# Two of the seven half-width products of a block, each pass of the large weight parts joined into one 512-column matmul

## The chip, the cores and the metric

The kernel runs on one core of a Trainium2 chip. The metric is the device time of one launch in microseconds (us). Three launches of the kernel before took 1768.8 to 1769.22 us, median 1769.01 us.

The engines are PE (matrix products, into PSUM), DVE (vector), ACT (scalar functions, also plain copies), POOL (GpSimd) and SP, which issues most transfers; POOL issues those transfers that add to what is already there.

## The reference

A decoder trunk of two layers on a 512 x 1024 activation in float32. Each layer is a gated feed-forward block (ffn), a token mixer and a second ffn, so there are four ffns in all, and they hold most of the time:

```python
def swiglu(h, w_gate, w_up, w_down):
    return (jax.nn.silu(h @ w_gate) * (h @ w_up)) @ w_down

for l in range(L):
    x = x + 0.5 * swiglu(rms_norm(x, ffn1_norm[l]), ffn1_w_gate[l], ffn1_w_up[l], ffn1_w_down[l])
    ...   # convolution and differential attention, joined by one output projection
    x = x + 0.5 * swiglu(rms_norm(x, ffn2_norm[l]), ffn2_w_gate[l], ffn2_w_up[l], ffn2_w_down[l])
```

The inner width of an ffn is 2816, that is 22 chunks of 128.

## The kernel before

**Split operands.** Each float32 operand is split in two parts that the PE takes: a high part `hi` (ACT copies it, L101 for weights) and a low part `lo` (DVE subtracts, L102; POOL in a few places of the mixer). A product of a weight chunk and an activation is three matmuls: high by high, high weight by low activation, low weight by high activation. L200, L203 and L204 are these three at 512 columns.

**Seven products.** Where the plain scheme would do eight half-width products, the kernel does seven, on weight combinations and activation combinations. This is done for the up and gate projections (`seven`, 16 of them in an ffn) and for the down projection (`Pair`, 8 in an ffn). The 22 chunks of an ffn are taken in three parts (`PARTS`): six chunks in the plain way at 512 columns, then a part of 8 sevens and 4 pairs, then another of 8 sevens and 4 pairs. So there are 64 sevens and 32 pairs in a launch. At the end of an ffn the first products of what follows begin two activation tiles in, before the last pair is finished (`first_products` with a `tail`), and take the eight tiles of `x` in the order 0, 4, 1, 5, 2, 6, 3, 7.

**One seven.** It has two PSUM banks of 512 columns, each used as two halves of 256: `a`, `d` in `banks[0]` and `b`, `c` in `banks[1]`. A product is four chunks of three matmuls of 256 columns (L434), 12 in all, accumulated in one of the halves; `go` names the half, the weight combination and the activation combination. In program order they are c, d, then `before()`, which is the last product of the seven before it (`rest`, weight `g1u1`), then a, b, c and a (weight `g1u2u1`). Between them ACT copies halves of the banks to the tile `keep` (four slots of 256 columns; L439, L443, L448), so that differences of accumulated states can be taken later, and DVE adds them back in (L451, L456, L457), ACT takes SiLU (L452), and DVE forms the gated product (L460). `Hidden.add` then splits that (L483 on ACT, L484 on DVE) and makes its combinations (L489 to L494).

**One pair** follows the same pattern for the down projection (matmuls at L523): `head`, `body` and `finish`. `finish` does the last product and adds to the running `x` (L572, L573, L574); the body adds its own half at L565 and L566. `finish_halves` serves the very last pair of the launch. After each finished `x` tile, `Prep.tile` splits it for the next products (L308 on ACT, L309 on DVE, L321 for the sum of squares).

**Order.** A scheduler turns the program into one instruction stream per engine; each stream runs in order, with semaphores between engines. Weights pass through rings of SBUF buffers (5 raw, 4 sums, 9 high, 9 low). A group of seven weight combinations is made ahead of its seven: four loads, two sums by a load on SP and a load on POOL's queue that adds to it (L160), two sums on DVE (L175, L176), seven splits (L101 on ACT and L102 on DVE).

Of the kernel before, what the change touches and what calls it, by code (L numbers as in the profile page):

```python
# [11 lines left out]
F32 = mybir.dt.float32  # L12
F32R = mybir.dt.float32r
I32 = mybir.dt.int32
AF = mybir.ActivationFunctionType
# [55 lines left out]
def trunk(ctx: ExitStack, tc: tile.TileContext, xt, par, lamv, relb, onehot,  # L71
# [12 lines left out]
    def f32(ap):  # L84
        return ap.bitcast(F32)
# [120 lines left out]

    x = act.tile([P, KT, SEQ], F32, tag="x", name="x")

    acth = act.tile([P, KT, SEQ], F32R, tag="acth", name="acth")
    actl = act.tile([P, KT, SEQ], F32R, tag="actl", name="actl")  # L210
# [11 lines left out]
    S.activation(small.tile([P, 1], F32, tag="first", name="first", bufs=1), f32(ones_r[:, P : P + 1]), AF.Copy)  # L222
# [152 lines left out]
    class Halves:  # L375
# [4 lines left out]
        def __init__(self, fp, pr, r):  # L380
            self.th = fp.tile([P, 3, KT // 2, HS], F32R, tag="th", name="th")
            self.tl = fp.tile([P, 3, KT // 2, HS], F32R, tag="tl", name="tl")

            self.whole = []
            four = [fp.tile([P, 4, SEQ], F32, tag=tag, name="hn") for tag in ("yh", "yl")]
            free = [t[:, n] for t in four for n in range(4)]
            a, b = slice(0, HS), slice(HS, SEQ)
            for j in range(KT // 2):
                for k in (j, j + KT // 2):
                    h = free.pop()  # L390
                    V.scalar_tensor_tensor(h, x[:, k, :], col(pr.l, pr.gain, k), r, op0=ALU.mult, op1=ALU.mult)
                    self.whole.append((k, h))
                (_, ha), (_, hb) = self.whole[-2:]
                t = fp.tile([P, 3, HS], F32, tag="ht", name="ht", bufs=1)
                V.tensor_tensor(t[:, 1], hb[:, b], ha[:, b], op=ALU.subtract)
                V.tensor_tensor(ha[:, b], ha[:, a], ha[:, b], op=ALU.subtract)
                V.scalar_tensor_tensor(t[:, 0], ha[:, b], -1.0, hb[:, b], op0=ALU.mult, op1=ALU.subtract)
                V.scalar_tensor_tensor(t[:, 2], t[:, 0], -1.0, hb[:, a], op0=ALU.mult, op1=ALU.subtract)
                S.activation(self.th[:, :, j, :], t, AF.Copy)
                V.tensor_tensor(self.tl[:, :, j, :], t, f32(self.th[:, :, j, :]), op=ALU.subtract)  # L400
# [16 lines left out]
    def seven(halves, w, banks, fp, before, last):  # L417
# [7 lines left out]
        g = keep[:, 0::2]  # L425
# [11 lines left out]

        go(c, "u2u1", "t1", first=True)
# [4 lines left out]
        S.activation(keep[:, :2], banks[0].rearrange("p (n c) -> p n c", n=2), AF.Copy)  # L443
        go(b, "g2", "b21")
        if not last:
            go(c, "all", "b22")
        go(a, "g1u2u1", "t2")
        saves.append(S.activation(keep[:, 2], a, AF.Copy))  # L448
        if last:
            go(c, "all", "b22")  # L450
# [14 lines left out]
    class Hidden:  # L465

        def __init__(self, fp, n):
            self.fp, self.n, self.parts = fp, n, [None] * (2 * n)
            self.th = fp.tile([P, 3, n, HS], F32R, tag="yh", name="yh")
            self.tl = fp.tile([P, 3, n, HS], F32R, tag="yl", name="yl")  # L470
# [33 lines left out]
    class Pair:  # L504

        def __init__(self, hid, fp, m, m2):
            self.hid, self.m, self.m2 = hid, m, m2
            self.kc, self.kd = (1, 3) if m == 0 else (3, 1)
            self.banks = pair_banks()
            self.a, self.d = self.banks[0][:, :HS], self.banks[0][:, HS:]  # L510
            self.b, self.c = self.banks[1][:, :HS], self.banks[1][:, HS:]
            self.keep = fp.tile([P, 4, HS], F32, tag="gn", name="keep", bufs=2)
            self.begun = set()
# [19 lines left out]
        def body(self, w, before, more=None, last=False):  # L533
            a, b, c, d, go = self.a, self.b, self.c, self.d, self.go
            both = self.banks[0].rearrange("p (n c) -> p n c", n=2)
            if self.m == 0:
# [13 lines left out]
                saves.append(S.activation(self.keep[:, 2:], both, AF.Copy))  # L550
            else:
# [4 lines left out]
                self.early = S.activation(self.keep[:, :2], both, AF.Copy)  # L556
                go(b, w["g2"], "b21")
                if not last:
                    go(c, w["all"], "b22")
                go(a, w["g1u2u1"], "t2")  # L560
                saves.append(S.activation(self.keep[:, 2], a, AF.Copy))
# [3 lines left out]
            V.tensor_tensor(two, two, self.keep[:, 0::2], op=ALU.add)  # L565
            V.scalar_tensor_tensor(xm, self.banks[1], 0.5, xm, op0=ALU.mult, op1=ALU.add)  # L566
            return nxt

        def finish(self, weight):
            a, d, xn = self.a, self.d, x[:, self.m2, :]  # L570
            self.go(a, weight, "t3")
            V.tensor_tensor(d, a, self.keep[:, self.kc], op=ALU.add)  # L572
            V.tensor_tensor(a, a, self.keep[:, self.kd], op=ALU.add)  # L573
            V.scalar_tensor_tensor(xn, self.banks[0], -0.5, xn, op0=ALU.mult, op1=ALU.add)  # L574

        def finish_halves(self, weight, store):
            a, xs = self.a, x[:, self.m2, :].rearrange("p (n c) -> p n c", n=2)
            V.scalar_tensor_tensor(xs, self.keep[:, 1::2], -0.5, xs, op0=ALU.mult, op1=ALU.add)
# [173 lines left out]
    def make_scalars():  # L752
        for l in range(DEPTH):
# [5 lines left out]
            d = small.tile([P, 2], F32, tag="lamd", name="lamd", bufs=1)  # L759
            V.tensor_reduce(d, pr, axis=AX.X, op=ALU.add)  # L760
            e = small.tile([P, 2], F32, tag="lame", name="lame", bufs=1)
# [428 lines left out]
```

## Time and profile before

| | before |
|---|---|
| median of 3 launches | 1769.01 us |
| profiled launch, its own time | 1769.0 us |
| span of that launch | 1767.2 us |
| PE busy | 1758.8 us, 11852 matmuls |
| DVE busy | 1472.1 us (83% of the span) |
| ACT busy | 1037.1 us (59%) |
| POOL busy | 515.7 us (29%) |

The profiled launch has 1.8 us outside its span and agrees with the median. Instructions on one engine are pipelined, so the durations of rows next to each other overlap a little, and those of matmuls much: a matmul's interval is the distance between starts and not its duration.

### The profile page before, as it was taken

How to read it: one execution, taken by the hardware profiler on the slowest of the kernel's cores; microseconds unless marked ns; L12 is line 12 of the kernel's file. 1: busy time of each engine (PE TensorE's matmuls, PEld its weight loads, DVE VectorE, ACT ScalarE, POOL GpSimd, SP SyncE). 2: the span in 40 equal slices, each digit the busy share in tenths (PEclk: the TensorE clock that was granted, in tenths of full speed). 3: DMA queues.
4: the chain of work that ended last, by engine and by line, in shares of the span. 5: the costliest groups of instructions: out<-in, count | busy, mean ns of one | idle time of the engine just before them, and what ended most of it. 6: DMA issues, size and time to landing. Idle time of an engine off the chain costs nothing.

```text
span 1767.2 us, 32964 instructions
## 1 busy us (share of the span) xinstructions
PE 1758.8 (100%) x11852; PEld 1621.2 (92%) x11852; DVE 1472.1 (83%) x2646; ACT 1037.1 (59%) x1955; POOL 515.7 (29%) x497
## 2 busy tenths in 40 slices
PE   9999999999999999999999999999999999999998
PEld 7799999988788899999988999999887888999998
DVE  7969888969877969989987798999698678698887
ACT  6546566755865436566644565666559554465664
POOL 1011112169970011212200121121798600112122
PEclk9999999999999999999999999999999999999999
DMA  7457777533223457677544576776231234576774
GB/s 229 129 138 185 172 188 190 138 120 100 68 78 114 126 129 178 171 198 179 141 143 111 147 177 172 198 166 166 91 114 49 96 102 139 134 183 163 201 183 127
DMA packets 166613, 257.78 MB, mean 146 GB/s; under 512 B 19271, under 2 KB 63318, under 8 KB 166448
## 3 DMA queue, kind: packets, MB, share of 16 engines
q1 hardware_dynamic: 129600, 201.25, 35.5%
q0 software_dynamic: 36416, 54.12, 18.7%
q8 instruction: 93, 1.52, 0.4%
q14 instruction: 72, 0.59, 0.1%
q10 hardware_dynamic: 432, 0.29, 0.1%
HBM read 253.48 MB, written 3.42 MB: 145 GB/s over the span
## 4 chain that ended last, share of the span: by engine, by line
PE 97%; DVE 1%; POOL 1%; ACT 1%; issue 0%; DVEq 0%; POOLq 0%
PE ps_pair L434 37%; PE ps_pair L523 18%; PE ps_pair L200 9%; PE ps_pair L203 9%; PE ps_pair L204 9%; PE ps_out L200 2%; PE ps_out L203 2%; PE ps_out L204 2%; PE ps_pair L842 2%; PE ps_pair L843 2%; PE ps_pair L841 2%; PE ps_sc L958 1%; PE ps_v L872 1%; PE ps_v L873 1%; PE ps_v L871 1%; POOL wlo L102 0%
## 5 line engine op out<-in xcount | busy, mean ns | idle before, releaser
L101 ACT ACTIVATE whi<-wraw 128x512 fp32r<-128x512 f32 x744 | 452.9, 627 | 397.4 <-PE ps_pair L203 166.3
L102 DVE TENSOR_TENSOR wlo<-wraw,whi 128x512 fp32r<-128x512 f32 x640 | 426.2, 685 | 111.5 <-ACT whi L101 104.2
L160 POOL DMA_DIRECT2D wsum<-in_gu x128 | 112.0, 904 | 700.4 <-DMA wsum<-in_gu 270.7
L434 PE MATMUL ps_pair<-acth,wlo 128*128 128x256 f32 x1024 | 289.8, 283 | 0.0
L434 PE MATMUL ps_pair<-actl,whi 128*128 128x256 f32 x1024 | 289.8, 283 | 0.0
L434 PE MATMUL ps_pair<-acth,whi 128*128 128x256 f32 x1024 | 289.8, 283 | 0.0
L434 PE MATMUL ps_pair<-th,whi 128*128 128x256 f32 x768 | 217.3, 283 | 0.0
L434 PE MATMUL ps_pair<-tl,whi 128*128 128x256 f32 x768 | 217.3, 283 | 0.0
L434 PE MATMUL ps_pair<-th,wlo 128*128 128x256 f32 x768 | 217.3, 283 | 0.0
L200 PE MATMUL ps_pair<-acth,whi 128*128 128x512 f32 x512 | 200.7, 394 | 0.3 <-DVE gs L653 0.3
L203 PE MATMUL ps_pair<-actl,whi 128*128 128x512 f32 x512 | 199.7, 390 | 0.0
L204 PE MATMUL ps_pair<-acth,wlo 128*128 128x512 f32 x512 | 199.3, 390 | 0.0
L434 PEld LDWEIGHTS ps_pair<-actl,whi 128*128 128x128 f32 x1024 | 196.6, 192 | 0.2
L434 PEld LDWEIGHTS ps_pair<-acth,whi 128*128 128x128 f32 x1024 | 196.6, 192 | 0.2
L434 PEld LDWEIGHTS ps_pair<-acth,wlo 128*128 128x128 f32 x1024 | 196.6, 192 | 0.0
L160 POOL DMA_DIRECT2D wsum<-in_dn x112 | 98.9, 1112 | 269.4 <-DMA wsum<-in_dn 55.7
L434 PEld LDWEIGHTS ps_pair<-th,whi 128*128 128x128 f32 x768 | 147.5, 192 | 0.0
L434 PEld LDWEIGHTS ps_pair<-tl,whi 128*128 128x128 f32 x768 | 147.5, 192 | 0.0
L434 PEld LDWEIGHTS ps_pair<-th,wlo 128*128 128x128 f32 x768 | 147.5, 192 | 0.0
L102 POOL TENSOR_TENSOR wlo<-wraw,whi 128x512 fp32r<-128x512 f32 x104 | 137.4, 1345 | 30.4 <-ACT whi L101 19.4
L523 PE MATMUL ps_pair<-hh,whi 128*128 128x256 f32 x512 | 144.9, 283 | 0.0
L523 PE MATMUL ps_pair<-hl,whi 128*128 128x256 f32 x512 | 144.9, 283 | 0.0
(209 smaller groups left out, 4446.5 us busy)
## 6 DMA issues: line engine op xcount, KB each, us to landing
wraw<-in_gu SPq DMA_DIRECT2D x280, 256.0 KB, 3.4
wsum<-in_gu SPq DMA_DIRECT2D x128, 256.0 KB, 3.7
wsum<-in_gu POOLq DMA_DIRECT2D x128, 256.0 KB, 4.7
wraw<-in_dn SPq DMA_DIRECT2D x68, 256.0 KB, 3.4
wraw<-in_wqkv SPq DMA_DIRECT2D x48, 256.0 KB, 2.7
wraw<-in_wout SPq DMA_DIRECT2D x48, 256.0 KB, 2.7
wraw<-in_dn SPq DMA_DIRECT2D x64, 128.0 KB, 4.0
wraw<-in_wag SPq DMA_DIRECT2D x32, 256.0 KB, 3.0
```

The costliest lines, as they stand in the source:

```text
L101: S.activation(hi, raw, AF.Copy)
L102: (eng or V).tensor_tensor(out=lo, in0=raw, in1=f32(hi), op=ALU.subtract)
L160: nc.gpsimd.dma_start(dst[:, to], src, accum_op=ALU.add)
L200: first = T.matmul(ps, wh, xh, start=start, stop=False)
L203: T.matmul(ps, wh, xl, start=False, stop=False)
L204: T.matmul(ps, wl, xh, start=False, stop=stop)
L434: mm = T.matmul(ps, l, r, start=first and i == j == 0, stop=False, skip_group_check=True)
L523: mm = T.matmul(ps, s[:, f], r, start=side not in self.begun, stop=False, skip_group_check=True)
L841: T.matmul(ps[n], xh[:, t], wh, start=k == 0, stop=False)
L842: T.matmul(ps[n], xh[:, t], wl, start=False, stop=False)
L843: T.matmul(ps[n], xl[:, t], wh, start=False, stop=k == KT - 1)
L871: T.matmul(ps, xh[:, t], wh, start=k == 0, stop=False)
```

## The change

In a `seven`, the product of weight `g1u2u1` (into a) and the product of weight `g1u1` (into a, in `rest`) are done by `both_columns`. For each chunk the large weight part meets the high and the low activation part in one matmul of 512 columns: the high one's product is accumulated in a, the low one's in d, the other half of the same bank. The low weight part by the high activation part stays one matmul of 256 columns into a. So 3 matmuls of 256 columns become one of 512 and one of 256. For this the high and low parts lie in one tile (`ts`; `ys` for pairs; `acts` for the activation). The same is done in the pairs' `finish`, and in `body` for all pairs but the first of each four and the very last.

Half d now holds a part of a product besides what it held. What d had before is known from an earlier copy, so the added part is taken out by more copies and sums: two ACT copies where there was one (L462 and L463 for L448), three POOL instructions of 128 x 256 (L456, L464, L465) in a seven, one more ACT copy in `rest` (L473). In the pairs these are L604, L593 and L594 on POOL, L591 and L592 in place of one copy, and L614 in `finish`. The streams have 728 matmuls fewer (11701 to 10973), 182 ACT instructions more and 269 POOL instructions more (228 to 497); DVE's sums keep their number.

```diff
+    def both_columns(bank, w, x, pin):
+        (wh, wl), (xh, both) = w, x
+        mm = T.matmul(bank.rearrange("p (n c) -> p n c", n=2), wh, both, start=False, stop=False, skip_group_check=True)
...
+        T.matmul(bank[:, :HS], wl, xh, start=False, stop=False, skip_group_check=True)
...
     # class Halves (class Hidden alike, with tag "ys")
-            self.th = fp.tile([P, 3, KT // 2, HS], F32R, tag="th", name="th")
-            self.tl = fp.tile([P, 3, KT // 2, HS], F32R, tag="tl", name="tl")
+            self.ts = fp.tile([P, 2, 3, KT // 2, HS], F32R, tag="ts", name="ts")
+            self.th, self.tl = self.ts[:, 0], self.ts[:, 1]
...
     # seven
+        def wide(wt, n):
+            for j in range(KT // 2):
+                t = halves.ts[:, :, n, j, :]
+                both_columns(banks[0], wpart([w[wt]], j), (t[:, 0], t), pin=j == 0)
...
         S.activation(keep[:, :2], banks[0].rearrange("p (n c) -> p n c", n=2), AF.Copy)
+        G.tensor_tensor(keep[:, 3], keep[:, 3], keep[:, 1], op=ALU.subtract)
...
-        go(a, "g1u2u1", "t2")
+        wide("g1u2u1", 0)
+        low = fp.tile([P, HS], F32, tag="low", name="low", bufs=1)
+        S.activation(low, d, AF.Copy)
         saves.append(S.activation(keep[:, 2], a, AF.Copy))
+        G.tensor_tensor(keep[:, 1], low, keep[:, 1], op=ALU.subtract)
+        G.tensor_tensor(keep[:, 2], keep[:, 2], keep[:, 1], op=ALU.add)
...
         def rest(out=None):
-            go(a, "g1u1", "t3")
+            wide("g1u1", 1)
+            S.activation(keep[:, 1], d, AF.Copy)
+            V.tensor_tensor(a, a, keep[:, 1], op=ALU.add)
             V.tensor_tensor(d, a, keep[:, 3], op=ALU.add)
-            V.tensor_tensor(a, a, keep[:, 1], op=ALU.add)
...
     # Pair.body, for the pairs with the wide product
                 self.early = S.activation(self.keep[:, :2], both, AF.Copy)
+                if not last:
+                    self.difference()
...
+                    low, sum2 = self.keep[:, self.kd], self.keep[:, 2]
+                    copy = self.fp.tile([P, HS], F32, tag="low", name="low", bufs=1)
+                    S.activation(copy, d, AF.Copy)
+                    saves.append(S.activation(sum2, a, AF.Copy))
+                    G.tensor_tensor(low, copy, low, op=ALU.subtract)
+                    G.tensor_tensor(sum2, sum2, low, op=ALU.add)
...
+        def difference(self):
+            kc = self.keep[:, self.kc]
+            G.tensor_tensor(kc, kc, self.keep[:, self.kd], op=ALU.subtract)
...
         def finish(self, weight):
-            self.go(a, weight, "t3")
+            self.wide(weight, 1)
+            S.activation(self.keep[:, self.kd], d, AF.Copy)
+            V.tensor_tensor(a, a, self.keep[:, self.kd], op=ALU.add)
             V.tensor_tensor(d, a, self.keep[:, self.kc], op=ALU.add)
-            V.tensor_tensor(a, a, self.keep[:, self.kd], op=ALU.add)
```

Lines move down with it: L451 becomes L468, L456 and L457 become L474 and L475 in the other order, L460 becomes L478, L484 becomes L502, L565 and L566 become L598 and L599, L572 to L574 become L615 to L617, L309 becomes L316, L321 becomes L328.

Three places in the streams. The first is DVE in the first part of the first ffn, around the sum that ends a seven (`wlo` is a weight's low part, `hl` that of a finished hidden chunk, the number behind a name counts tiles). Before:

```order
L484 TENSOR_TENSOR hl_1572<-hid_1554,hh_1571 128x512 [waits Activation_49]
L451 TENSOR_TENSOR ps_pair_1527<-ps_pair_1527,keep_1528 128x512 [waits Activation_49]
L102 TENSOR_TENSOR wlo_1792<-wsum_1635,whi_1791 128x512 [waits DMASW2_49,PE_49,Activation_49]
L102 TENSOR_TENSOR wlo_1796<-wraw_1777,whi_1795 128x512 [waits DMAHW1_49,PE_49,Activation_49]
L102 TENSOR_TENSOR wlo_1800<-wraw_1779,whi_1799 128x512 [waits DMAHW2_49,PE_49,Activation_49]
L456 TENSOR_TENSOR ps_pair_1526<-ps_pair_1526,keep_1528 128x256 [waits PE_49]
```

And in the changed kernel:

```order
L102 TENSOR_TENSOR wlo_1781<-wsum_1626,whi_1780 128x512 [waits DMASW2_49,PE_49,Activation_49]
L502 TENSOR_TENSOR hl_1562<-hid_1547,hh_1561 128x512 [waits Activation_49]
L468 TENSOR_TENSOR ps_pair_1520<-ps_pair_1520,keep_1521 128x512 [waits Pool_49]
L102 TENSOR_TENSOR wlo_1785<-wraw_1766,whi_1784 128x512 [waits DMAHW1_49,PE_49,Activation_49]
L102 TENSOR_TENSOR wlo_1789<-wraw_1768,whi_1788 128x512 [waits DMAHW2_49,PE_49,Activation_49]
L102 TENSOR_TENSOR wlo_1793<-wraw_1770,whi_1792 128x512 [waits DMAHW3_49,PE_49,Activation_49]
L175 TENSOR_TENSOR wraw_1773<-wsum_1626,wraw_1768 128x512
L474 TENSOR_TENSOR ps_pair_1519<-ps_pair_1519,keep_1521 128x256 [waits Activation_49]
```

The sum L468 waits for POOL where L451 waited for ACT, one weight split has moved ahead of it, and the first sum of `rest` (L474) waits for ACT where L456 waited for PE.

The second place is POOL's stream in the same stretch. Before, it held only the transfers that add to a weight sum:

```order
L160 DMA wsum_1490<-in_gu1 128x512 [waits DMASW4_49,DMAHW2_49,DVE_49,Activation_49]
L160 DMA wsum_1493<-in_gu1 128x512 [waits DMASW5_49,DMAHW3_49,DMASW1_49,DVE_49]
L160 DMA wsum_1635<-in_gu1 128x512 [waits DMASW6_49,DMAHW7_49,DVE_49,Activation_49]
L160 DMA wsum_1638<-in_gu1 128x512 [waits DMAHW0_49,DMASW7_49,DVE_49]
L160 DMA wsum_1785<-in_gu1 128x512 [waits DMASW0_49,DMAHW4_49,DVE_49,Activation_49]
```

And in the changed kernel:

```order
L456 TENSOR_TENSOR keep_1373<-keep_1373 128x256 [waits Activation_49]
L464 TENSOR_TENSOR keep_1373<-low_1468,keep_1373 128x256 [waits Activation_49,Pool_49]
L160 DMA wsum_1626<-in_gu1 128x512 [waits DMAHW7_49,DMASW6_49,DVE_49]
L465 TENSOR_TENSOR keep_1373<-keep_1373 128x256 [waits Activation_49,Pool_49]
L160 DMA wsum_1629<-in_gu1 128x512 [waits DMAHW0_49,DMASW7_49,DVE_49]
L456 TENSOR_TENSOR keep_1521<-keep_1521 128x256 [waits Activation_49]
L464 TENSOR_TENSOR keep_1521<-low_1611,keep_1521 128x256 [waits Activation_49,Pool_49]
L465 TENSOR_TENSOR keep_1521<-keep_1521 128x256 [waits Activation_49,Pool_49]
```

The three sums of a seven stand between the transfers, in some sevens with a transfer between the second and the third.

The third place is DVE at the end of the first ffn, where the last pair is finished and the last tiles of `x` are split for the mixer. Before:

```order
L572 TENSOR_TENSOR ps_pair_4480<-ps_pair_4480,keep_4482 128x256 [waits PE_49]
L102 TENSOR_TENSOR wlo_4803<-wraw_4800,whi_4802 128x512 [waits DMAHW5_49,Activation_49]
L309 SCALAR_TENSOR_TENSOR actl_77<-x_75,par0_78,acth_76 128x512 [waits Activation_49]
L573 TENSOR_TENSOR ps_pair_4480<-ps_pair_4480,keep_4482 128x256 [waits DVE_49]
L321 TENSOR_TENSOR ssum_4146<-ssum_4146,sq_4582 128x512 [waits Activation_49]
L574 SCALAR_TENSOR_TENSOR x_75<-ps_pair_4480,x_75 128x512 [waits DVE_49]
L309 SCALAR_TENSOR_TENSOR actl_77<-x_75,par0_78,acth_76 128x512 [waits Activation_49]
```

And in the changed kernel:

```order
L598 TENSOR_TENSOR ps_pair_4433<-ps_pair_4433,keep_4434 128x512 [waits Pool_49]
L615 TENSOR_TENSOR ps_pair_4432<-ps_pair_4432,keep_4434 128x256 [waits Activation_49]
L316 SCALAR_TENSOR_TENSOR acts_76<-x_75,par0_77,acts_76 128x512 [waits Activation_49]
L328 TENSOR_TENSOR ssum_4102<-ssum_4102,sq_4527 128x512 [waits Activation_49]
L599 SCALAR_TENSOR_TENSOR x_75<-ps_pair_4433,x_75 128x512 [waits DVE_49]
L102 TENSOR_TENSOR wlo_4750<-wraw_4747,whi_4749 128x512 [waits DMAHW5_49,Activation_49]
L616 TENSOR_TENSOR ps_pair_4432<-ps_pair_4432,keep_4434 128x256 [waits DVE_49]
L316 SCALAR_TENSOR_TENSOR acts_76<-x_75,par0_77,acts_76 128x512 [waits Activation_49]
L617 SCALAR_TENSOR_TENSOR x_75<-ps_pair_4432,x_75 128x512 [waits DVE_49]
L328 TENSOR_TENSOR ssum_4102<-ssum_4102,sq_4532 128x512 [waits Activation_49]
L316 SCALAR_TENSOR_TENSOR acts_76<-x_75,par0_77,acts_76 128x512 [waits Activation_49]
```

The body's sum of the last pair now waits for POOL right ahead of the finish, and eight DVE instructions stand between L615 and the last split where five stood between L572 and it.

More of the change, by code (lines that the diff above doesn't have):

```diff
@@ L221, in trunk @@
     V.tensor_copy(ones_r, fill)
-    S.activation(small.tile([P, 1], F32, tag="first", name="first", bufs=1), f32(ones_r[:, P : P + 1]), AF.Copy)
+    S.activation(small.tile([P, 1], F32, tag="r2", name="first"), f32(ones_r[:, P : P + 1]), AF.Copy)
     ones_r = ones_r[:, :P]
@@ L380, in __init__ @@
         def __init__(self, fp, pr, r):
-            self.th = fp.tile([P, 3, KT // 2, HS], F32R, tag="th", name="th")
-            self.tl = fp.tile([P, 3, KT // 2, HS], F32R, tag="tl", name="tl")
+            self.ts = fp.tile([P, 2, 3, KT // 2, HS], F32R, tag="ts", name="ts")
+            self.th, self.tl = self.ts[:, 0], self.ts[:, 1]
             self.whole = []
-            four = [fp.tile([P, 4, SEQ], F32, tag=tag, name="hn") for tag in ("yh", "yl")]
-            free = [t[:, n] for t in four for n in range(4)]
+            eight = fp.tile([P, 8, SEQ], F32, tag="ys", name="hn")
+            free = [eight[:, n] for n in range(8)]
             a, b = slice(0, HS), slice(HS, SEQ)
@@ L549, in body @@
                 go(a, w["g1u2u1"], "t2", rest)
-                saves.append(S.activation(self.keep[:, 2:], both, AF.Copy))
+                saves.append(S.activation(self.keep[:, 2:4], both, AF.Copy))
+                self.difference()
             else:
@@ L559, in body @@
                     go(c, w["all"], "b22")
-                go(a, w["g1u2u1"], "t2")
-                saves.append(S.activation(self.keep[:, 2], a, AF.Copy))
+                if last:
+                    go(a, w["g1u2u1"], "t2")
+                else:
+                    self.wide(w["g1u2u1"], 0)
+                if last:
+                    saves.append(S.activation(self.keep[:, 2], a, AF.Copy))
+                else:
+                    low, sum2 = self.keep[:, self.kd], self.keep[:, 2]
[4 more added lines that the diff above has]
+                    G.tensor_tensor(sum2, sum2, low, op=ALU.add)
                 if last:
@@ L577, in finish_halves @@
             a, xs = self.a, x[:, self.m2, :].rearrange("p (n c) -> p n c", n=2)
-            V.scalar_tensor_tensor(xs, self.keep[:, 1::2], -0.5, xs, op0=ALU.mult, op1=ALU.add)
+            V.scalar_tensor_tensor(xs, self.keep[:, 1:4:2], -0.5, xs, op0=ALU.mult, op1=ALU.add)
             self.go(a, weight, "t3")
```

24 lines of the change are left out of this document (16 added, 8 removed).

## The prediction

> **What bounds the kernel now.** I read the page's busy times first, then the chain of work that ended last.
>
> ```profile
> span 1767.2 us, 32964 instructions
> PE 1758.8 (100%) x11852; PEld 1621.2 (92%) x11852; DVE 1472.1 (83%) x2646; ACT 1037.1 (59%) x1955; POOL 515.7 (29%) x497
> PE 97%; DVE 1%; POOL 1%; ACT 1%; issue 0%; DVEq 0%; POOLq 0%
> ```
>
> PE is the bound: it is never idle, and 97% of the chain is PE. So every nanosecond that PE is spared counts, as long as nothing makes it wait. DVE at 83% is the next engine. The longest pieces of the chain give the price of a half-width matmul, and the chain just ahead of the first of them that of a full-width one.
>
> ```profile
> 99.86 0.23 PE ps_pair L200
> ...
> 107.12 0.23 PE ps_pair L204
> 107.34 80.63 PE ps_pair L434 x672
> 187.98 38.88 PE ps_pair L523 x324
> ```
>
> 80.63 us for 672 matmuls of 256 columns is 0.1200 us each (38.88 over 324 gives the same). Between 99.86 and 107.34 stand 33 matmuls of 512 columns, so 7.48 / 33 = 0.2267 us each. Two halves take 0.240, one whole 0.227: a matmul has a fixed share of some 13 ns. How full DVE is in the stretch of an ffn that the change touches, the windows say (columns: window, length, then busy time and instructions of PE, weight loads, DVE, ACT and POOL).
>
> ```profile
> 107.30:188.00 80.70, 80.70 (x675) 80.70 (x674) 69.51 (x121) 50.30 (x94) 14.41 (x17) 1.00 0.71 176
> 309.00:358.50 49.50, 49.50 (x378) 47.85 (x377) 47.09 (x82) 33.35 (x63) 9.95 (x15) 1.00 0.56 148
> 107.30:358.50 251.20, 251.20 (x2059) 249.56 (x2058) 224.61 (x391) 157.09 (x297) 48.74 (x60) 1.00 0.70 174
> ```
>
> The third row is everything from the first seven of an ffn to the end of its last pair. DVE idles 251.20 - 224.61 = 26.6 us of it; in eight sevens (first row) 11.2 us, 1.4 a seven; in the last four pairs with the end (second row) only 2.4 us.
>
> **The change, part by part.** *PE.* 64 sevens lose 8 matmuls, 31 finishes and 23 bodies lose 4: 512 + 124 + 92 = 728, as the streams have it. Each is a pair of 0.240 turned into one of 0.227, so 728 x 13 ns = 9.5 us, all on the path. The rivals below doubt this term and what stands against it.
>
> *ACT.* 182 more copies of 128 x 256 from PSUM, by the first of these rows 0.385 us each.
>
> ```profile
> L448 ACT ACTIVATE keep<-ps_pair 128x256 f32<-128x256 f32 x64 | 24.6, 385 | 44.8 <-PE ps_pair L434 44.8
> L451 DVE TENSOR_TENSOR ps_pair<-ps_pair,keep 128x512 f32<-128x512 f32 x64 | 44.4, 694 | 19.6 <-PE ps_pair L434 16.5 <-ACT keep L448 3.1
> L443 ACT ACTIVATE keep<-ps_pair 128x512 f32<-128x512 f32 x64 | 38.3, 598 | 58.7 <-PE ps_pair L434 58.7
> L452 ACT ACTIVATE keep<-ps_pair 128x512 f32<-128x512 f32 x64 | 37.8, 591 | 10.7 <-DVE ps_pair L451 10.7
> L913 POOL TENSOR_TENSOR yp<-yp,prod 128x512 f32<-128x512 f32 x78 | 101.2, 1298 | 7.2 <-ACT prod L912 4.5
> L1000 POOL TENSOR_TENSOR so<-so,se 128x4 f32<-128x4 f32 x8 | 1.6, 201 | 7.3 <-DVE so L999 7.3
> ```
>
> ACT has 157.09 of 251.20 us busy there; 46 copies in an ffn add 18 us. It costs nothing as throughput. Behind `rest`'s copy (L473) DVE has three splits and L175 ahead of L474, so that wait is covered as well.
>
> *POOL and L468's wait.* No row shows a POOL sum of 128 x 256. One of 128 x 512 takes 1.298 us, one of 128 x 4 takes 0.201: half the first is 0.65, the middle of the two 0.75. L468 is ready two copies and two sums after the wide product, 2 x 0.385 + 2 x 0.70 = 2.2 us, where L451 was one copy behind it. L468 then ends 2.9 us after that product (0.69 more). What is queued behind it on DVE are splits for the next group; what waits for it is ACT's SiLU (L452's row, 0.59), and behind that on ACT the copy of the next seven's `banks[0]` (L443's row, 0.60), which PE needs before the next `g1u2u1` product, six products or 8.6 us later. L468 may therefore end as late as 8.6 - 0.6 - 0.6 = 7.4 us after its product before PE waits: 4.5 us of cover, and this wait costs PE nothing. A transfer that stands between L464 and L465 could lengthen it (rival D).
>
> *POOL against DVE.* This is the term that decides. The trace shows the two working at once in the mixer only (first row: minimum, median and maximum of six; the others from the timeline, in start and length).
>
> ```profile
> L941 DVE SCALAR_TENSOR_TENSOR u<-th,u x6: 682/1772/1782, 503.9 to 1387.3; 128x512 f32<-128x512 f32 x6
> 506.58 1.77 DVE L941 SCALAR_TENSOR_TENSOR u<-th,u 128x512 f32<-128x512 f32 x1
> 508.27 0.41 DVE L1065 TENSOR_TENSOR x<-ps_out,x 128x256 f32<-128x256 f32 x1
> 506.05 3.45 POOL L102 TENSOR_TENSOR wlo<-wraw,whi 128x512 fp32r<-128x512 f32 x2
> 471.05 2.54 POOL L102 TENSOR_TENSOR wlo<-wraw,whi 128x512 fp32r<-128x512 f32 x2
> ```
>
> A DVE instruction with two SBUF inputs takes 0.68 us alone and 1.77 beside a running POOL sum: it waited 1.09 us, nearly the whole sum. POOL's pair of sums went from 2.54 to 3.45. A DVE instruction that reads PSUM and one SBUF tile took 0.41 us at 508.27, while the same pair of POOL sums ran: it is not held. So a POOL sum half as long can hold such a DVE instruction for half of 1.09, 0.55 us. The Trainium skill, "SBUF — State Buffer", section "Who interferes with whom", says that a DVE instruction with two SBUF inputs contends with a GpSimd instruction that reads SBUF, and with at most one it does not; the trace agrees in both halves (1.77 against 0.68, and 0.41 unchanged).
>
> Four DVE instructions of a seven read a PSUM bank and one SBUF tile; by the first window there are 121 / 8 = 15.1 in a seven, so 11.1 of them, 0.735, read two SBUF tiles. So a POOL sum costs the full 0.55 only if the instruction under way when it comes and the next one are both of that kind, 0.735 x 0.735 = 0.54; else a PSUM instruction of some 0.6 us (L451 takes 0.69 at 512 columns) covers most, I put 0.12 on it. b = 0.54 x 0.55 + 0.46 x 0.12 = 0.35 us. Bounds: 0.30 (cover complete) and 0.55 (no cover). Below 0.30 would need idle DVE at the right moment; a gain is excluded, since nothing is taken from DVE.
>
> An ffn has 16 x 3 + 6 x 3 + 2 = 68 such sums: 68 x 0.35 = 23.8 us of DVE time. There is room for 26.6 - 2.4 (PE's stretch is shorter by 9.5 / 4) = 24.2 us. It just fits, and it does not fit evenly: a seven has 1.3 us and needs 1.05, but the last four pairs have 2.4 and need 10 x 0.35 = 3.5, so DVE comes 1.1 us late to the end of the ffn. What is late there PE feels at once:
>
> ```profile
> 350.11 0.69 DVE L565 TENSOR_TENSOR ps_pair<-ps_pair,keep 128x512 f32<-128x512 f32 x1
> 353.71 0.42 DVE L572 TENSOR_TENSOR ps_pair<-ps_pair,keep 128x256 f32<-128x256 f32 x1
> 356.24 0.68 DVE L574 SCALAR_TENSOR_TENSOR x<-ps_pair,x 128x512 f32<-128x512 f32 x1
> 357.71 0.75 DVE L309 SCALAR_TENSOR_TENSOR actl<-x,par,acth 128x512 fp32r<-128x512 f32 x1 [0.80 <-ACT acth L308]
> 351.83 0.40 PE L200 MATMUL ps_pair<-acth,whi 128*128 128x512 f32 x1
> ```
>
> The last split ends at 358.46, and PE, which resumes full-width matmuls at 351.83 with the third tile, gets to the last tile 5 x 6 matmuls later, 351.83 + 30 x 0.227 = 358.64: a margin of 0.2 us. The finish's new copy and the three more DVE instructions behind L615 add some 0.4 (before, L572 ran 1.7 us after PE was through, being queued, so most is hidden). I take 1.1 + 0.4 = 1.5 us at each of the three ends that other products follow, 4.5 us; bounds 0.2 and, at b = 0.55, 13 us an end (68 x 0.55 - 24.2).
>
> *Sum*, against the profiled launch's own 1769.0 us (span 1767.2 and 1.8 around it; the median is 1769.01): 1769.0 - 9.5 + 4.5 = **1764.0 us**. The new tiles only share or replace SBUF; SP's stream keeps its order, so no load moves.
>
> **The rivals.** About 0.2% (3.5 us) is what a measurement of this kernel can tell from no change.
>
> *A, the forecast:* b at most 0.37, 1759.5 to 1765.5 us. For it: DVE's room, row by row. Against it: room is 24.2 and need 23.8, and DVE cannot use idle moments in which it waits for something.
>
> *B, slower: DVE becomes the bound through POOL's sums.* Place: the whole ffn, felt where PE waits for the last tiles of `x`. The time is 1769.0 - 9.5 + 3 x (68 b - 24.2): the gain is eaten at b = 0.40; b = 0.45 gives 1778.7, 0.50 gives 1788.9, 0.55 gives 1799. For it: the 1.77 us row, and that the next engine already works 224.61 of 251.20 us. Against: the PSUM cover. The same section of the skill says that whoever issues first holds the pair for the whole instruction; with the whole 0.70 us and no cover the formula would give 1830, but the 1.09 us wait beside sums of 1.30 is shorter than that.
>
> *C, the joined matmul saves little.* Its moving operand comes in two runs 256 columns apart in SBUF, and no row shows such a one. If it takes 0.240, the time is 1769.0 + 4.5 = 1773.5. The Trainium skill, "TensorE: Matmul & The Clock Gate", section "Back-to-back issue gap", gives N / 2.4 + 2.5 ns for an isolated gap, 109 and 216 ns: joining would save 2.5 ns, 1.8 us in all, and 1771.7. The rows of this trace, 120 and 227, speak for 13 ns.
>
> *D, the waits eat the gain:* a weight transfer queued ahead of L465 holds POOL, L468 waits on POOL, and DVE stands with its splits queued behind. One such wait of 0.1 to 0.2 us in each seven takes 3 to 8 us more, or b lies at 0.38 to 0.42: 1765.5 to 1772.5.
>
> **How the numbers follow.** A 0.43, B 0.39, C 0.06, D 0.12. Faster is A, 0.43; the same is D and C's upper half (0.04), 0.16; slower is B and the rest of C, 0.41. The likeliest case is A, at 1764.0, own range 1759.5 to 1765.5. Cases of both signs hold most of the chance, so the range reaches from A's low end, 1759.5, to b = 0.50 in B, 1790: beyond lies about a third of B, 0.13, and below 0.05.
>
> **What would show it.** Right: the long pieces of L434 are gone, the chain shows joined matmuls at 0.227 and halves at 0.120, a seven's period is 60 x 0.120 + 8 x 0.227 + 8 x 0.120 = 9.98 us (84 x 0.120 = 10.08 before), PE waits only at three ends, for 1 to 2 us. The POOL sums take 0.65 to 0.75 and DVE's splits next to them now and then 1.2 instead of 0.68. B shows as PE idle inside the sevens or of many us at the ends, released by DVE, with DVE at 95% or more. C shows as joined matmuls 0.24 apart. D shows as L468 waiting on POOL while POOL's idle time is released by a DMA. Wrong altogether would be a time outside the range, or a gain with DVE's room untouched: then the conflict costs less than 0.30.

## The result and the profile after

The changed kernel takes 1842.59 us (median; 1841.63 to 1846.88), the kernel before 1768.9 in the same comparison: 1.0421 times, interval 1.0408 to 1.0434. It is slower by 74 us, where 1764.0 was forecast with a range from 1759.5 to 1790.

The page of the changed kernel: span, busy times, and the chain that ended last.

```profile
span 1840.6 us, 32301 instructions
PE 1778.2 (97%) x11124; PEld 1593.4 (87%) x11124; DVE 1592.6 (87%) x2646; ACT 1072.9 (58%) x2137; POOL 779.8 (42%) x766
PE 64%; DVE 19%; ACT 5%; DMA 5%; issue 4%; POOL 2%; SPq 0%; DVEq 0%; POOLq 0%; ACTq 0%
```

DVE has the same 2646 instructions and is busy 1592.6 instead of 1472.1 us, 120.5 more. PE falls from 97% of the chain to 64%, and DVE holds 19% of it. The windows show where (columns as in the prediction; the eight sevens of the first block, the four pairs behind them, and the second block of sevens).

```profile
106.90:193.20 86.30, 81.43 (x609) 77.49 (x608) 78.94 (x120) 51.74 (x108) 37.92 (x41) 1.00 0.67 159
193.20:232.40 39.20, 39.16 (x302) 37.73 (x301) 37.07 (x59) 23.90 (x49) 13.73 (x16) 1.00 0.70 173
236.70:322.90 86.20, 80.35 (x586) 75.93 (x585) 81.22 (x126) 51.88 (x110) 41.36 (x44) 0.98 0.74 175
```

The first eight sevens take 86.3 us where they took 80.7, with DVE busy 78.94 of it where it was busy 69.51. Taken over all eight such blocks (from the start of the first to the start of the last matmul of each), the sevens grew from 632.6 to 693.8 us, the pairs' blocks (at three ends only up to the pause before the last pair's `finish`) from 311.5 to 322.0, and those three pauses by 2.0: 61.2 + 10.5 + 2.0 = 73.7, against 73.4 us between the two spans. Most of the loss is in the sevens.

The 0.98 in the last row is the granted clock of PE. Five stretches of 3.4 us in this launch, one of them in that window, have a clock of 0.50, and matmuls of 256 columns come 0.213 us apart in them instead of 0.120. PE had idled 1.9 to 2.5 us in the 3.4 us ahead of each. The kernels in which PE hardly waits (before, and without the sums) have none. By this order the stretches follow from the waits; at half the clock they cost at most half their length, 8.5 us in all.

Who holds whom in the sevens, the groups and the waits tell (groups: busy us, mean ns; waits: us in all, times, longest).

```profile
L102 DVE TENSOR_TENSOR wlo<-wraw,whi 128x512 fp32r<-128x512 f32 x640 | 465.3, 746 | 75.6 <-ACT whi L101 71.5 <-PE ps_pair L203 2.0 <-PE ps_pair L441 0.7
L102 DVE TENSOR_TENSOR wlo<-wsum,whi 128x512 fp32r<-128x512 f32 x192 | 162.1, 860 | 18.6 <-ACT whi L101 18.6
L176 DVE TENSOR_TENSOR wraw<-wraw 128x512 f32<-128x512 f32 x96 | 84.9, 884 | 0.7
L468 DVE TENSOR_TENSOR ps_pair<-ps_pair,keep 128x512 f32<-128x512 f32 x64 | 44.0, 688 | 19.3 <-POOL keep L465 17.3 <-PE ps_pair L441 2.0
L464 POOL TENSOR_TENSOR keep<-low,keep 128x256 f32<-128x256 f32 x64 | 69.8, 1091 | 209.8 <-ACT low L462 209.8
```

```profile
ACT whi L101 <- DVE wraw L176: 144.3, 74, 3.9
ACT keep L469 <- DVE ps_pair L468: 79.7, 56, 2.8
PE ps_pair L209 <- ACT keep L455: 29.4, 19, 2.8
ACT keep L473 <- POOL keep L465: 21.5, 18, 3.4
DVE ps_pair L468 <- POOL keep L465: 17.3, 9, 3.6
PE ps_pair L209 <- ACT keep L463: 15.8, 20, 1.7
```

DVE's instructions with two SBUF inputs in these rows (682 to 685 ns before) now take 746 to 884 ns on the mean, while L468, which reads PSUM and one SBUF tile, stays at 688. PE waits at the first joined matmul (L209) of `g1u2u1` for the copy L455; in 15 of the 19 waits (23.3 of 29.4 us) ACT reached that copy late because L469 ahead of it waited for DVE's L468. That is the way from a late DVE to PE that the prediction described and thought covered by 4.5 us. There is a second way, which it did not name: the joined product of `rest` waits for the copy L463, and in 17 of 20 waits (13.3 us) ACT was late there because it had waited for a weight sum of DVE (L176) to split. Waits for POOL itself are the smaller part. Of the 51 us that PE waits at joined matmuls, 9 have one right ahead (ACT's L473 or DVE's L468, both for L465); in the rest DVE had done at least eleven instructions in a row without waiting for anyone.

### The profile page after: what moved, and what is told of

It is laid out like the page before. It is cut to its first block, busy times and chain, and to the rows that moved or that the text cites. A ratio compares the mean times of both kernels' runs of the same rounds, so it can differ in the third digit from the quotient of the medians.

```text
span 1840.6 us, 32301 instructions
## 1 busy us (share of the span) xinstructions
PE 1778.2 (97%) x11124; PEld 1593.4 (87%) x11124; DVE 1592.6 (87%) x2646; ACT 1072.9 (58%) x2137; POOL 779.8 (42%) x766
## 4 chain that ended last, share of the span: by engine, by line
PE 64%; DVE 19%; ACT 5%; DMA 5%; issue 4%; POOL 2%; SPq 0%; DVEq 0%; POOLq 0%; ACTq 0%
PE ps_pair L441 10%; PE ps_pair L204 9%; PE ps_pair L200 9%; PE ps_pair L203 9%; PE ps_pair L542 8%; DVE wlo L102 7%; PE ps_pair L209 5%; DMA wsum<-in_gu 3%; PE ps_pair L212 2%; ACT whi L101 2%; DVE wraw L175 2%; DVE wraw L176 2%; PE ps_out L200 2%; PE ps_out L203 2%; PE ps_out L204 2%
## 5 line engine op out<-in xcount | busy, mean ns | idle before, releaser
L102 DVE TENSOR_TENSOR wlo<-wraw,whi 128x512 fp32r<-128x512 f32 x640 | 465.3, 746 | 75.6 <-ACT whi L101 71.5
L441 PE MATMUL ps_pair<-acts,whi 128*128 128x256 f32 x2048 | 377.0, 285 | 0.2 <-ACT keep L451 0.2
L441 PEld LDWEIGHTS ps_pair<-acts,whi 128*128 128x128 f32 x2048 | 320.4, 192 | 6.7 <-ACT keep L451 0.4
L441 PE MATMUL ps_pair<-acts,wlo 128*128 128x256 f32 x1024 | 291.5, 285 | 0.0
L209 PE MATMUL ps_pair<-ts,whi 128*128 128x512 f32 x512 | 194.9, 414 | 45.6 <-ACT keep L455 29.4
L200 PE MATMUL ps_pair<-acts,whi 128*128 128x512 f32 x512 | 200.6, 395 | 0.2 <-DVE gs L696 0.2
L204 PE MATMUL ps_pair<-acts,wlo 128*128 128x512 f32 x512 | 200.2, 392 | 0.6 <-DVE wlo L102 0.6
L203 PE MATMUL ps_pair<-acts,whi 128*128 128x512 f32 x512 | 200.1, 391 | 0.0
L441 PEld LDWEIGHTS ps_pair<-acts,wlo 128*128 128x128 f32 x1024 | 196.7, 192 | 0.0
L102 DVE TENSOR_TENSOR wlo<-wsum,whi 128x512 fp32r<-128x512 f32 x192 | 162.1, 860 | 18.6 <-ACT whi L101 18.6
L209 PEld LDWEIGHTS ps_pair<-ts,whi 128*128 128x128 f32 x512 | 98.1, 192 | 73.5 <-ACT keep L455 33.5
L464 POOL TENSOR_TENSOR keep<-low,keep 128x256 f32<-128x256 f32 x64 | 69.8, 1091 | 209.8 <-ACT low L462 209.8
L542 PE MATMUL ps_pair<-hh,wlo 128*128 128x256 f32 x512 | 145.5, 284 | 0.0
L212 PE MATMUL ps_pair<-ts,wlo 128*128 128x256 f32 x512 | 145.5, 284 | 0.0
```

The lines of the kernel that those rows point to most:

```text
L102: (eng or V).tensor_tensor(out=lo, in0=raw, in1=f32(hi), op=ALU.subtract)
L200: first = T.matmul(ps, wh, xh, start=start, stop=False)
L203: T.matmul(ps, wh, xl, start=False, stop=False)
L204: T.matmul(ps, wl, xh, start=False, stop=stop)
L209: mm = T.matmul(bank.rearrange("p (n c) -> p n c", n=2), wh, both, start=False, stop=False, skip_group_check=True)
L212: T.matmul(bank[:, :HS], wl, xh, start=False, stop=False, skip_group_check=True)
```

## Experiments

Each change is against the changed kernel. "DVE per sum" below is DVE's busy time over the eight blocks of sevens, less the 552.8 us it has there without any sum, over the number of sums in them.

**No sums.** All six `G.tensor_tensor` lines removed, three in the sevens (shown) and three in the pairs:

```diff
-        G.tensor_tensor(keep[:, 3], keep[:, 3], keep[:, 1], op=ALU.subtract)
-        G.tensor_tensor(keep[:, 1], low, keep[:, 1], op=ALU.subtract)
-        G.tensor_tensor(keep[:, 2], keep[:, 2], keep[:, 1], op=ALU.add)
```

> The changed kernel without its 269 POOL sums (L456, L464, L465, L604, L593, L594 left out, so the output is not the reference's); joined matmuls, ACT copies and the new order of DVE's sums stay. Theory 1 (the POOL sums hold DVE's SBUF reads and make DVE the bound) and theory 2 (DVE waits for the chain copy, POOL sum, POOL sum, with weight transfers in POOL's queue) both expect the loss to be gone: 1769 less what joining saves, by the trace of the changed kernel 236 + 117 ns for a joined matmul and its partner against 3 x 120, 7 ns x 728 = 5 us: 1764, and at most 1769 with waits at the three ends. Theory 3 (joining itself, or the 182 copies on ACT, make PE wait) expects 1800 or more.

1763.21 us, 0.9968 of before (0.9955 to 0.9982). The whole loss hangs on the sums; joining, the 182 copies and the new order bring 5.7 us. A joined product in this kernel, from its chain of waits:

```profile
118.93 0.23 PE ps_pair L209
119.16 0.12 PE ps_pair L212
...
120.21 0.12 PE ps_pair L212
120.34 4.31 PE ps_pair L441 x36
```

Four joined steps take 120.34 - 118.93 = 1.41 us, 352 ns each against 3 x 120: 7.5 ns saved, not 13, and 728 x 7.5 = 5.5 us.

**Fills in place of sums**, one and three. A fill stands where a sum stood and is waited for in the same way, but reads nothing:

```diff
-        G.tensor_tensor(keep[:, 1], low, keep[:, 1], op=ALU.subtract)
-        G.tensor_tensor(keep[:, 2], keep[:, 2], keep[:, 1], op=ALU.add)
+        G.memset(low, 0.5)             # once, or three times
+        G.memset(keep[:, 2], 0.5)
...                                     # the other four sums alike
```

> The changed kernel with a fill of the same 128x256 tile in place of each POOL sum: it stands at the same place in POOL's queue, waits for the same ACT copies and the same instructions wait for it, but it reads no SBUF (the output is not the reference's). Theory 1 (DVE is held by POOL's reads) expects about what the kernel without the sums takes, 1764 to 1772. Theory 2 (the wait through POOL's queue) expects most of the loss to stay, less what a fill is shorter than a sum: 1800 to 1840.

1767.31 us with one, 0.9992 (0.998 to 1.0003).

> Three fills of 128x256 one after the other in place of each POOL sum (a fill took 0.31 to 0.64 us in the run with one; the output is not the reference's): POOL's part of the chain that DVE's L468 waits for is then about as long as in the changed kernel, where a sum takes 1.09 us, but nothing on POOL reads SBUF. Theory 1 (DVE held by POOL's reads) expects 1767 to 1778. Theory 2 (the length of the chain through POOL) expects 1800 to 1842.

1777.19 us with three, 1.0039 (1.0025 to 1.0052). POOL is busy 741.0 us in it, nearly the 779.8 of the changed kernel, yet DVE's busy time is that of before. So a chain through POOL of this length costs PE 14 us against the kernel without sums, and not 79.

**Sums into a scratch tile.** The same reads, but nothing reads the results:

```diff
-        G.tensor_tensor(keep[:, 1], low, keep[:, 1], op=ALU.subtract)
-        G.tensor_tensor(keep[:, 2], keep[:, 2], keep[:, 1], op=ALU.add)
+        G.tensor_tensor(low, low, keep[:, 1], op=ALU.subtract)
+        G.tensor_tensor(low, keep[:, 2], keep[:, 1], op=ALU.add)
...                                     # the other four sums alike
```

> The changed kernel with the POOL sums reading the same tiles, but writing to a tile that no engine reads, so that DVE and ACT no longer wait for POOL (the output is not the reference's). Theory 1 expects nearly the whole loss to stay, 1825 to 1842. Theory 2 expects the loss to go: 1764 to 1780.

1826.46 us, 1.0327 (1.0297 to 1.0357). For theory 1, but not cleanly: ACT's SiLU overwrites a slot of `keep` and waited 41 us for POOL's reads, and a copy in the pairs waited 29 us. The next run takes most of that away.

**Sums beside the work**, three, two and one of them in each seven and pair (L456 and L604 left out, the pairs' other sums changed alike):

```diff
-        G.tensor_tensor(keep[:, 1], low, keep[:, 1], op=ALU.subtract)
-        G.tensor_tensor(keep[:, 2], keep[:, 2], keep[:, 1], op=ALU.add)
+        G.tensor_tensor(low, low, keep[:, 3], op=ALU.subtract)
+        G.tensor_tensor(low, low, keep[:, 3], op=ALU.add)      # not with one
+        G.tensor_tensor(low, low, keep[:, 3], op=ALU.add)      # only with three
```

> Three POOL sums behind the copy of d in each seven and pair, reading and writing only that copy and a slot of keep that is not written again (the output is not the reference's). The kernel with sums into a scratch tile (1826.46) still had ACT's SiLU and a copy wait for POOL's reads, 41 and 29 us of waiting in its trace; here no engine waits for a sum until the next seven's copy of d, 8 us later. Theory 1 expects the loss to stay all the same: 1810 to 1830. Theory 2 expects 1764 to 1772.

Three: 1845.75 us, 1.0434 (1.0412 to 1.0456). No engine uses these sums, and the loss is the whole loss, above the 1830 that theory 1 expected at most. One wait for POOL is left: ACT's next copy of d waited for the last sum 8 times, 22.1 us in all, and 4.2 us of PE's waits come through it. That is too little for 82 us, so theory 2 falls: the hold of DVE by POOL's reads is enough for a loss of this size. It lies in part elsewhere, though. Against the kernel without sums, the sevens lose 48 us and the pairs' blocks 35, where the changed kernel loses 65 and 12.

> As the kernel with three sums beside the work (1845.75), but one POOL sum for each seven and pair instead of three (the output is not the reference's). In the sevens of the changed kernel a sum cost DVE 0.49 us (94.6 us more DVE time for 192 sums). If the loss is a balance, DVE's hold against the 1.2 us of a seven in which DVE idles, one sum (0.5 us) fits and PE does not wait: 1763 to 1770. If every hold delays PE by its own length, wherever it falls, a third of the loss stays: (1845.75 - 1763.2) / 3 = 27.5, 1791.

One: 1763.71 us, 0.9971 (0.9959 to 0.9984), nothing lost.

> Two POOL sums beside the work for each seven and pair, where one took 1763.71 and three took 1845.75 (the output is not the reference's). With one sum a seven DVE's busy time in the sevens rose by 12.0 us for 64 sums, 0.19 us each, against 0.53 each with three. If the hold stays small as long as DVE keeps idle moments and grows once it lags, two sums stand at the edge: 128 x 0.19 = 24 us of the 75.6 us idle would leave PE alone, 1764 to 1767; 128 x 0.5 = 64 us would fill it nearly, 1780 to 1800. If the loss is in proportion to the sums beyond the first, 1805.

Two: 1780.46 us, 1.0067 (1.0044 to 1.009), at the low end of the second case. The same window of the first block with none, one, two and three sums a seven:

```profile
107.00:187.50 80.50, 80.50 (x611) 77.52 (x611) 69.03 (x121) 54.51 (x109) 14.72 (x17) 1.00 0.71 174
```

```profile
107.00:187.50 80.50, 80.50 (x613) 77.60 (x612) 70.49 (x122) 54.45 (x110) 20.75 (x24) 1.00 0.72 176
```

```profile
107.00:187.50 80.50, 80.50 (x613) 77.60 (x613) 74.91 (x120) 52.67 (x108) 28.66 (x33) 1.00 0.69 169
```

```profile
107.00:187.50 80.50, 77.08 (x579) 73.27 (x578) 76.90 (x112) 49.69 (x104) 29.60 (x35) 1.00 0.66 158
```

PE's first number is full (80.50) until the third row; with three sums DVE is at 76.90 of 80.50 and PE falls back. With two the sevens are 4.3 us longer over all blocks, and most of the loss is in the pairs' blocks (324.9 us, 310.3 without sums). Over all blocks DVE per sum is 0.19, 0.36 and 0.53 us for one, two and three: (564.8, 599.0, 654.7) - 552.8, over 64, 128 and 192 sums. The hold of a sum is no constant. The share of the sums beside which a DVE instruction gets over 0.1 us longer goes the same way: 34, 76 and 88%. Why one is nearly free shows in a seven of the kernel with one, DVE first and then POOL:

```profile
126.25 0.69 DVE L466 TENSOR_TENSOR ps_pair<-ps_pair,keep 128x512 f32<-128x512 f32 x1
126.86 0.68 DVE L102 TENSOR_TENSOR wlo<-wsum,whi 128x512 fp32r<-128x512 f32 x1
```

```profile
126.02 0.92 POOL L463 TENSOR_TENSOR low<-low,keep 128x256 f32<-128x256 f32 x1 [6.60 <-ACT low L461]
```

The sum runs beside the PSUM sum (L466, which is L468), both being released by copies of the same product, and is through when the next split starts. Once DVE lags, it does splits at that time, as in the changed kernel:

```profile
171.58 2.38 DVE L102 TENSOR_TENSOR wlo<-wsum,whi 128x512 fp32r<-128x512 f32 x2
176.89 1.60 DVE L175 TENSOR_TENSOR wraw<-wsum,wraw 128x512 f32<-128x512 f32 x1
```

```profile
171.11 1.16 POOL L464 TENSOR_TENSOR keep<-low,keep 128x256 f32<-128x256 f32 x1 [4.81 <-ACT low L462]
172.34 1.07 POOL L465 TENSOR_TENSOR keep<-keep 128x256 f32<-128x256 f32 x1
176.88 1.05 POOL L456 TENSOR_TENSOR keep<-keep 128x256 f32<-128x256 f32 x1
```

Two splits beside L464 and L465 take 2.38 us (1.28 undisturbed), and L175 beside L456 takes 1.60 (0.68).

**Corrections without joining.** `both_columns` does three matmuls of 256 columns into a:

> The changed kernel with all copies and sums, but three matmuls of 256 columns again instead of a joined one and one of 256; the low product is then not in d, the difference L464 makes is zero, and the output is right. What joining alone is worth in this kernel: theories 1 and 2 have DVE or the chain as the bound, so PE's 5 us more hardly show, 1840 to 1848; theory 3 (joining costs more than it saves) expects clearly less than 1842, down to 1769.

1843.1 us, 1.0421 (1.0391 to 1.0451), as theories 1 and 2 had it: with DVE as the bound, what PE saves by joining is not seen.

**The sums on DVE.** The two behind the joined product read PSUM, so the copies go; the difference L456 becomes a DVE instruction as it stands, and the pairs are changed alike:

```diff
-        S.activation(low, d, AF.Copy)
-        saves.append(S.activation(keep[:, 2], a, AF.Copy))
-        G.tensor_tensor(keep[:, 1], low, keep[:, 1], op=ALU.subtract)
-        G.tensor_tensor(keep[:, 2], keep[:, 2], keep[:, 1], op=ALU.add)
+        V.tensor_tensor(keep[:, 1], d, keep[:, 1], op=ALU.subtract)
+        saves.append(V.tensor_tensor(keep[:, 2], a, keep[:, 1], op=ALU.add))
```

> The changed kernel with its sums on DVE instead of POOL, two of the three read straight from PSUM, so that the two ACT copies behind the g1u2u1 product go as well (the output is right). DVE gets 269 more instructions of 128x256, 0.35 us each by their distance in the trace: as much DVE time in an ffn, 68 x 0.35 = 24 us, as the prediction put on the hold, and no POOL sum. If the prediction's balance was sound and only the hold's size was off (theory 1a), 1764 to 1770. If DVE's idle time cannot be filled that far, whatever fills it (theory 1b), 1785 to 1830.

1797.16 us, 1.0159 (1.0137 to 1.0181): theory 1b, at its lower part. DVE gains 59.7 us in the sevens for 192 instructions, 0.31 each and less than the prediction's 0.35 for a hold, and their blocks are 13.8 us longer than without sums, the rest being lost in the pairs and at the ends. By the balance these 59.7 us fit into 75.6 of idle time. But this is no clean test of it, for PE's longest wait in this kernel is this:

```profile
PE ps_pair L209 <- DVE keep L588: 10.2, 6, 2.4
```

The next longest is the same wait for L462 in the sevens, 7.1 us. L588 and L462 are moved sums themselves: PE's next joined product, which had waited for an ACT copy in that place, now waits for DVE's queue. The run shows that the place of an added instruction counts besides its length; how much of the 34 us is missing room, it does not show.

**Only the last product joined**, its difference on DVE (first run, the last two sums and their copies gone, `g1u2u1` narrow), on POOL (second), and on DVE with the pairs as before (third):

```diff
-        wide("g1u2u1", 0)
+        go(a, "g1u2u1", "t2")
...
-        G.tensor_tensor(keep[:, 3], keep[:, 3], keep[:, 1], op=ALU.subtract)
+        V.tensor_tensor(keep[:, 3], keep[:, 3], keep[:, 1], op=ALU.subtract)   # G in the second
```

> Only the last of the seven products is joined, in sevens and in finish; the g1u2u1 product is three matmuls of 256 columns again, its two copies and two sums go, and the one difference that is left (L456, L604) is on DVE. The output is right. 380 joined matmuls save 7 ns each, 2.7 us; 95 DVE instructions of 0.35 us are 24 x 0.35 = 8 us in an ffn, a third of DVE's idle time. 1766 by theory 1a and by theory 2; 1769 to 1775 by theory 1b.

1786.79 us, 1.0099 (1.0081 to 1.0118), outside what either theory expected.

> Only the last of the seven is joined, in sevens and in finish, with its one difference (L456, L604) on POOL as in the changed kernel; the output is right. 380 joined matmuls save 7.5 ns each, 2.9 us. By the balance, one sum in a seven or pair fits: 1766 to 1770. If every hold delays PE: 95 x 0.49 = 47 us more, 1813. The kernel with the same difference on DVE took 1786.79, all of its loss in the pairs' own products behind the last seven of a block.

1769.77 us, 1.0007 (0.9998 to 1.0016): no change that can be told, and 3.8 us short of what 380 joined steps of 7.5 ns save.

> Only the last product of the sevens is joined, its difference on DVE; the pairs are those of the kernel before, with narrow products and no difference. The output is right. The sevens of the kernel with that change in both took 1.5 us less than before and the pairs 20 us more, so without the pairs' part: 1769 - 256 x 7.5 ns = 1767, if the pairs' loss came from their own difference and copy; 1780 or more if it came from the last seven of a block (its copy and sum ahead of the hidden chunk that the pairs wait for).

1788.66 us, 1.0114 (1.01 to 1.0128): taking the pairs' part away did not help. So the loss is not that of the pairs' own difference and copy; it is the second case that was expected. The loss of the first and third lies at the end of each block of sevens. The third kernel's DVE there, and then the second's:

```profile
185.95 0.70 DVE L464 TENSOR_TENSOR ps_pair<-ps_pair,keep 128x512 f32<-128x512 f32 x1 [2.04 <-PE ps_pair L441]
186.56 0.68 DVE L474 SCALAR_TENSOR_TENSOR hid<-ps_pair,keep 128x512 f32<-128x512 f32 x1
189.51 0.68 DVE L498 TENSOR_TENSOR hl<-hid,hh 128x512 fp32r<-128x512 f32 x1
```

```profile
183.13 0.69 DVE L474 SCALAR_TENSOR_TENSOR hid<-ps_pair,keep 128x512 f32<-128x512 f32 x1
185.98 0.70 DVE L464 TENSOR_TENSOR ps_pair<-ps_pair,keep 128x512 f32<-128x512 f32 x1 [1.70 <-PE ps_pair L441]
186.59 0.68 DVE L498 TENSOR_TENSOR hl<-hid,hh 128x512 fp32r<-128x512 f32 x1
```

In the third kernel the hidden chunk of the last but one seven (L474) stands in DVE's stream behind L464, which waits 2 us for PE's last product, and so L498 comes at 189.51 and not at 186.59; the pairs wait for it. In the second it stands ahead. DVE idles 2.04 us there, so by these lines it is the scheduler's order at that place, and not DVE's load, that makes most of those 20 us; no run changed the order alone. No version of these is faster than the kernel before beyond what its measurement can tell.

## Why the prediction was wrong, step by step

*The saving.* 9.5 us was mis-sized: the row of plain 512-column matmuls (227 ns) was taken for one whose moving operand and result lie in two halves, and a joined step saves 7.5 ns, not 13. The kernel without sums gives 5.7 us in all. Rival C named this doubt and put 0.06 on it; it was half right. This step alone would have moved the time by some 4 us.

*The hold, b = 0.35.* Its size when it happens was right: beside a sum of the changed kernel, DVE instructions with two SBUF inputs are longer by 0.54 us at the median of those held, where 0.55 was worked out. Its chance was not: 0.54 was taken from a random meeting, and 86% of the 269 sums in the changed kernel hold one. b is (647.4 - 552.8) / 192 = 0.49 us in the sevens, where 0.35 was put. The chance depends on the load itself, as the row of one, two and three sums shows: 0.19, 0.36, 0.53. A cost that grows with the lag that it makes can't be put into a balance as a constant. The lock for the whole instruction, which rival B takes from the Trainium skill, "SBUF — State Buffer", section "Who interferes with whom", is told there of DVE's two-port modes; the 0.54 us measured here is about half of a sum's 1.07 us.

*The room, 24.2 us an ffn.* This step failed most. It counted every idle moment of DVE as fillable. The sevens of the changed kernel have 94.6 us more DVE work than those without sums (647.4 - 552.8), and 75.6 us were idle there: a balance with the right hold would still have lost only 19 us in them. They lost 65.3 (693.8 - 628.5), because 46.4 us (693.8 - 647.4) stay idle. Of those, 17.3 are L468's wait for POOL, and some 20 are waits for ACT's high parts. Even with three sums beside the work, where DVE waits for POOL nowhere in the sevens, 22 us stay idle (676.9 - 654.7). DVE works in order, and part of its idle time is waiting for ACT's copies of products and splits that are not there yet, which a busier DVE meets again. The run with the sums on DVE points the same way, but PE waits for the moved sums themselves in it.

*Where it would be felt.* The prediction had 4.5 us at the three ends: the pauses there grew by 2.0 us. "A seven has 1.3 us and needs 1.05", and 4.5 us of cover: the sevens, which it took as safe, lost 61.2 us. The cover is there once, and a deficit in each seven uses it up; from then on PE waits at L209 as shown above. Working out the cover was right, and using it against a lag that adds up was not. The way over L176, ACT's split and the copy L463 has no cover worked out at all.

*L468's wait for POOL.* "Costs PE nothing" nearly stands up at the length of single fills (1767.31, 4 us over no sums), less well at three (14 us over no sums). How much the changed kernel's chain adds to the hold stays open: 9 of PE's 51 us of waits at joined matmuls have a wait for POOL right ahead, but three sums beside the work cost as much as the sums in the chain. Rival D had this wait and the transfer queued ahead of L465; its 3 to 8 us do not follow from 0.1 to 0.2 us in each of 64 sevens, which is 6.4 to 12.8.

*Rival B* had the mechanism, DVE made the bound by POOL's sums, and its sign. Its formula, at the measured b of 0.49, gives 1759.5 + 3 x (68 x 0.49 - 24.2) = 1786.9 us. It is 56 us short, mostly because it took the same fillable room from the need; that it let the rest be felt at three ends instead of in all four ffns is worth only 9 of them.

## What to carry to other kernels

An engine that is 86% busy in a stage has not 14% to give: ask for each idle moment what it waits for, and count as room only what would still be idle if everything came later by the added work. Work put on an idle engine is not free if it shares something with the next busiest one; there, test it first with the added instructions alone, on data that nobody waits for, at one, two and three times the amount. And price a merged instruction from a row with the same operand layout, or take the saving as an interval.

## What the runs showed of the hardware

- A POOL sum of two 128x256 tiles in SBUF takes 0.735 us at the median where no DVE instruction with two SBUF inputs runs beside it (the kernels with sums beside the work), and 1.07 at the median in the changed kernel, where such a DVE instruction gets 0.54 us longer: both sides wait for each other. A DVE instruction that reads PSUM was never longer beside one (9 ns at most, of 92 in the changed kernel).
- POOL fills of the same tiles (three for each sum, POOL busy 741.0 us) left DVE's busy time at 1465.8 us, where the kernel without sums has 1469.7. The Trainium skill, "SBUF — State Buffer", section "Who interferes with whom", says that DVE instructions with two SBUF inputs contend with a GpSimd instruction that reads SBUF and not with one that only writes it. These two runs agree.
- A joined matmul of 512 columns, with operand and result in two halves, followed by one of 256 columns, takes 352 ns, where plain ones of those sizes take 227 and 120.
- After a wait of PE of about 2 us the changed kernel's trace shows stretches of 3.4 us at a granted clock of 0.50, five in the launch, with matmuls of 256 columns 0.213 us apart instead of 0.120.
